# A two-layer hybrid decoder: the diagonal of linear attention as an elementwise product, small matmuls on all 128 rows, and other code for the first and the last norm

## The chip, the cores and the metric

The kernel runs on one core of one Trainium2 chip. The metric is the time of one execution on the device, in microseconds (us).

## The reference

The input x has 512 tokens of 1024 channels in float32. There are two layers. Each adds a mixer (a state-space scan, "SSD"; gated linear attention, "GLA"; dilated window attention; all three fed by one input projection and merged by sigmoid gates) and a gated MLP with a short convolution. An RMSNorm stands before each of these and at the end. Comments at the right are added here.

```python
def rmsnorm(x, w):
    xf = x.astype(jnp.float32)
    y = xf * lax.rsqrt(jnp.mean(xf * xf, axis=-1, keepdims=True) + RMS_EPS)
    return (y * w.astype(jnp.float32)).astype(x.dtype)

def gla_chunked(q, k, v, log_a):                 # q, k: 4 heads of 64; v: 4 heads of 128
...
    bcum = jnp.cumsum(log_a.reshape(bsz, nc, C, nh, dk), axis=2)
    causal = jnp.tril(jnp.ones((C, C), dtype=bool))
    diff = bcum[:, :, :, None] - bcum[:, :, None, :]
    decay = jnp.exp(jnp.where(causal[:, :, None, None], diff, -jnp.inf))
    scores = jnp.einsum('bcthd,bcshd,bctshd->bchts', q, k, decay)
    o_intra = jnp.einsum('bchts,bcshe->bcthe', scores, v)
...
def gla_mixer(q, k, v, gate_lr, r, gate_w, gate_b, norm_w):
...
    pre = gate_lr.astype(f32) @ gate_w.astype(f32) + gate_b.astype(f32)   # 16 rows to 256
    log_a = (jax.nn.log_sigmoid(pre) / GLA_TAU).reshape(bsz, seq, GLA_HEADS, GLA_DK)
    o = gla_chunked(qh, kh, vh, log_a)
...
def hybrid_mixer(hn, ...):
    proj = hn @ w_in.astype(hn.dtype)
    (z, xbc, dt_raw, gq, gk, gv, g_lr, g_r, qkv, gates) = jnp.split(...)
    y_ssd = ssd_mixer(z, xbc, dt_raw, ...)       # dt_raw: 16 columns
    y_gla = gla_mixer(gq, gk, gv, g_lr, g_r, ...)
    y_att = dilated_attention_mixer(qkv)
    merged = (gates[:, :, 0] * (y_ssd @ wb_ssd) + gates[:, :, 1] * (y_gla @ wb_gla)
              + gates[:, :, 2] * (y_att @ wb_att))
    return merged @ w_out.astype(hn.dtype)
...
def reference(x, ...):
    for l in range(DEPTH):                       # 2
        x = x + hybrid_mixer(rmsnorm(x, norm1_w[l]), ...)
        x = x + conv_ffn(rmsnorm(x, norm2_w[l]), ...)
    return rmsnorm(x, final_norm_w)
```

In the scores of GLA a token's own term (t = s) has decay 1, so the diagonal of the scores is the sum over d of q[t,d] * k[t,d].

## The kernel before

**Layout.** Activations lie with channels on the 128 partitions and the 512 tokens along the free side: x is eight tiles of 128x512 (xs). float32 products of full size are done in three passes of a rounded format: each operand is split into a high part (wh, xh) and the remainder (wl, xl), and `mm3` issues high by high, low by high, high by low. All weights are read in the order of use as 374 units of 128x1024 (`weight_plan`). `fetch` loads a unit, `parts` splits it (cast wh on ACT, subtraction wl on DVE), `unit` hands it to the projection that uses it; a unit is split two units ahead, and there are three buffers of wh and of wl, so a cast waits until PE is through with an older unit. A unit is 24 matmuls of 128x512.

**Order.** The order on PE is that of the code: the large matmuls of a unit are queued in a list (`large`), and each small matmul, issued by `mm` or `transpose`, is followed by one large one. Work beside the projections is written as generators (`side`), which are advanced by `tick` when a unit's matmuls have been queued; a generator says by `yield n` after how many units it wants to go on. The rows of ACT, DVE, POOL and SP are placed by the framework's scheduler; each engine works its row in order. Small matmuls are plain float32, and a profile shows each as two passes.

**The places of the change.** `small_proj` makes gd: rows 0 to 15 are the low-rank input of the GLA gate, rows 32 to 47 the raw step sizes of SSD; the other rows of the weight unit are zero. `gla_decay` multiplies rows 0 to 15 with the gate weights gw. `ssd_decay` transposes rows 32 to 47, four blocks of 128 tokens. `gla_pair` handles two heads (64 rows each); there are two pairs in a layer, started one unit apart. It begins with five clears on DVE (suf, two ksb, two qsb) and the diagonal: eight products of k and q over the 64 rows of a head, masked with the identity into S; later levels write the blocks below the diagonal into S.

`norm_stats` sums the squares by matmuls with ones, `factors` computes the reciprocal root (three Newton steps on 128x4 or 128x8 tiles) and four diagonal tiles dg; one unit later `norm_side` broadcasts the factors to all partitions by a matmul of ones with dg and copies them to rstdB. `first` loads x and makes the first split and the squares. The last norm does the same without a side, multiplies each tile of x by the broadcast in PSUM on DVE, and writes it out from two queues, ACT's (even tiles) and SP's (odd).

Of the kernel before, what the change touches and what calls it, by code (L numbers as in the profile page):

```python
# [11 lines left out]
F32 = mybir.dt.float32  # L12
# [84 lines left out]
def shape_constants():  # L97
# [22 lines left out]
    is_b = (i[:, None] // 32 == np.arange(4)[None, :]).astype(f)  # L120
    own = np.stack([is_r, is_b], axis=1)
    own64 = np.concatenate([i[:, None] % 16 == np.arange(16)[None, :],
                            i[:, None] % 64 // 16 == np.arange(4)[None, :]], axis=1).astype(f)
    lev = np.zeros((P, 7, 64), f)
    for n in range(7):
        L = 1 << n
# [10 lines left out]
def hybrid_decoder(ctx: ExitStack, tc: tile.TileContext, ins, out):  # L137
# [19 lines left out]
    def big(shape, dt=F32, n="b"):  # L157
        return big_p.tile(shape, dt, tag="b", name=nm(n))
# [128 lines left out]
    def blk(c):  # L287
        return slice(c * P, (c + 1) * P)
# [12 lines left out]
    for l in range(depth):  # L301
        pcs.append(cp.tile([P, N_PC], F32, name=f"pc{l}"))
        rows.append(cp.tile([P, 48], F32, name=f"rows{l}"))
        gws.append(cp.tile([16, 256], F32, name=f"gw{l}"))
    fnw = cp.tile([P, KD], F32, name="fnw")
    ident, tri, strict = mats[:, 0], mats[:, 1], mats[:, 2]
    own64 = cp.tile([P, 20], F32, name="own64")
    own_c = cp.tile([P, 4, P], F32R, name="own_c")
    ones = cp.tile([P, P], F32, name="ones")
    V.memset(ones, 1.0)  # L310

    def constants():
        for t, n in ((mats, "mats"), (own64, "own64"), (amask, "amask"), (sel, "sel"), (own, "own"), (fnw, "fnw")):
            nc.sync.dma_start(out=t, in_=ins[n])
        for l in range(depth):
            if l:
                nc.sync.dma_start(out=pcs[l], in_=ins["pc"][l])
            nc.sync.dma_start(out=rows[l], in_=ins["rows"][l].partition_broadcast(P))
            nc.sync.dma_start(out=gws[l], in_=ins["gw"][l])
        levf = big([P, 7, 64], n="levf")  # L320
        nc.sync.dma_start(out=levf, in_=ins["lev"])
        for n in range(7):
            V.tensor_copy(lev[:, n].rearrange("p (c i) -> p c i", c=4), levf[:, n:n + 1].to_broadcast([P, 4, 64]))
        V.tensor_copy(own_c, own64[:, 16:20].unsqueeze(2).to_broadcast([P, 4, P]))
# [38 lines left out]
    def norm_stats(acc, both):  # L363

        n = 8 if both else 4
        ss = mx()
        for c in range(n):
            mm(ss[:, c:c + 1], acc[:, blk(c) if c < 4 else res(c - 4)], ones[:, 0:1], True, True)
        return factors(ss, n)

    def factors(ss, n):
        t = sml([P, n])
        V.tensor_scalar(t, ss[:, :n], 1.0 / D, EPS, ALU.mult, ALU.add)
        rsqrt(rs[:, :n], t, n)
        if n == 8:
            V.tensor_scalar(hr, rs[:, :4], 0.5, None, ALU.mult)
        dg = big([P, T], n="dg")
        for c in range(4):
            V.tensor_scalar(dg[:, blk(c)], ident, rs[:, c:c + 1], None, ALU.mult)
        return dg  # L380

    def norm_side(acc, both):
        dg = norm_stats(acc, both)
        yield 1
        b = mx()
        mm(b, ones, dg, True, True)
        A.copy(rstdB, b)


    def attention(yh, yl, pre):  # L390
# [144 lines left out]
    def small_proj():  # L535
        o = pp()
        proj_cm(o, xhl, "small")
        gd = big([64, T], n="gd")
        V.tensor_mul(gd, o[:64], rstdB[:64])
        return gd  # L540


    def gla_decay(l, gd, las):
        pc, gw = pcs[l], gws[l]
        for m in range(2):
            o = mx()
            mm(o, gw[:, blk(m)], gd[:16], True, True)
            p0, p1 = big([P, T], n="p0"), big([P, T], n="p1")
            V.tensor_scalar(p0, o, pc[:, O_GB + m:O_GB + m + 1], None, ALU.add)
            V.tensor_scalar(p1, p0, 0.0, None, ALU.min)  # L550
            V.scalar_tensor_tensor(p0, p1, 2.0, p0, ALU.mult, ALU.subtract)
            las.append((p0, p1))
# [38 lines left out]
    def gla_pair(m, qk, cum, vt, wt, pc, yh, yl):  # L591
# [7 lines left out]
        hp = [slice(0, 64), slice(64, 128)]  # L599
        S = [big([P, 2, 2, P], n="S") for _ in range(2)]  # L600
        X = []
        for j in range(2):
            o = mx()
            for c in range(4):
                mm(o[:, blk(c)], k[hp[j], blk(c)], q[hp[j], blk(c)], True, True)
            for x in range(2):
                V.tensor_mul(S[x][:, :, j], o[:, 256 * x:256 * x + 256].rearrange("p (c t) -> p c t", c=2),
                             ident.unsqueeze(1).to_broadcast([P, 2, P]))
        for n in range(9):
            L = 1 << n  # L610
            G = 256 // L
# [81 lines left out]
    def ssd_decay(l, gd, dec):  # L693
# [3 lines left out]
        A.activation(nA, rw[:, 16:32], AF.Exp)  # L697
        o = mx()
        for c in range(4):
            transpose(o[:, 16 * c:16 * c + 16], gd[32:48, blk(c)], ident[32:48, 32:48])  # L700
        pre = sml([P, 4, 16], n="pre")
        V.tensor_add(pre, o[:, :64].rearrange("p (c h) -> p c h", c=4), rw[:, :16].unsqueeze(1).to_broadcast([P, 4, 16]))
        pre = pre.rearrange("p a b -> p (a b)")
        mn = sml([P, n], n="mn")
        V.tensor_scalar(mn, pre, 0.0, None, ALU.min)
# [343 lines left out]
    for c in range(4):  # L1049
        mm(ss[:, c:c + 1], sq[:, blk(c)], ones[:, 0:1], False, c == 3)  # L1050
    A.activation(xs[KD - 1], xs[KD - 1], AF.Copy, scale=fnw[:, KD - 1:KD])
    dg = factors(ss, 4)
    b = mx()
    mm(b, ones, dg, True, True)
    for m in range(KD):
        V.tensor_mul(xs[m], xs[m], b)  # L1056
        (nc.sync if m % 2 else A).dma_start(out=out[:, m], in_=xs[m])
    assert pos[0] == len(plan)

# [58 lines left out]
```

## Time and profile before

| what | value |
|---|---|
| median of 3 runs | 2325.44 us (2324.39 to 2331.16) |
| profiled execution, its own time | 2324.64 us |
| its span, first to last instruction | 2322.8 us |
| mean granted TensorE clock | 0.997 |
| busy: PE, PEld, DVE, ACT, POOL | 99%, 83%, 61%, 39%, 0% |
| matmuls (passes) | 10776 |
| read from HBM | 200.35 MB |

Busy time of PE is modelled from pipelined matmuls, so steps between starts say more than durations. An operation's row has its start, its duration, engine, line, operation, names (out<-in), shape and count; what stands in brackets is the idle time of the engine before it and what ended that. Matmuls and weight loads (PEld) are listed apart.

### The profile page before, as it was taken

The numbers are of one execution on the slowest core, as the hardware profiler recorded it, in microseconds if no ns is written. First come the engines' busy times: TensorE is split into PE (matmuls) and PEld (weight loads), VectorE is DVE, ScalarE is ACT, GpSimd is POOL, SyncE is SP. The second block draws the span as 40 slices with busy tenths as digits, with TensorE's granted clock in tenths as the row PEclk, the third lists the DMA queues.
The fourth block names the chain that finished last, engine by engine and source line by source line (L and its number), as shares of the span: only waits on it lengthen the run. The fifth ranks groups of instructions, "written<-read, shape, count | busy, mean of one in ns | idle before, by whom it ended". The sixth has DMA issues, their size and how long they took to land.

```text
span 2322.8 us, 27385 instructions
## 1 busy us (share of the span) xinstructions
PE 2299.9 (99%) x10776; PEld 1918.3 (83%) x10776; DVE 1412.0 (61%) x2511; ACT 901.9 (39%) x1487; POOL 0.2 (0%) x4
## 2 busy tenths in 40 slices
PE   8999999999999999999999999999999999999997
PEld 7888878888888888888898888788888888888886
DVE  4467548687865566654325764686888556665533
ACT  4344423445443333332224444234454433333321
POOL 0000000000000000000000000000000000000000
PEclk9999999999999999999999999999999999999998
DMA  5322222222223333233333222222222233333331
GB/s 180 102 82 75 80 64 91 76 71 73 82 75 98 92 98 97 94 100 96 95 91 100 82 82 68 74 85 73 73 73 82 82 94 97 95 97 100 95 96 54
DMA packets 58512, 204.21 MB, mean 88 GB/s; under 512 B 7152, under 2 KB 7824, under 8 KB 58384
## 3 DMA queue, kind: packets, MB, share of 16 engines
q1 hardware_dynamic: 57808, 201.42, 28.3%
q8 instruction: 84, 1.38, 0.2%
q10 hardware_dynamic: 576, 1.05, 0.1%
q14 instruction: 44, 0.36, 0.1%
HBM read 200.35 MB, written 2.10 MB: 87 GB/s over the span
## 4 chain that ended last, share of the span: by engine, by line
PE 98%; DVE 1%; ACT 0%; DMA 0%; issue 0%; DVEq 0%; SPq 0%; ACTq 0%
PE pp L178 77%; PE pp L183 11%; PE mx L186 8%; PE mx L190 1%; DVE wl L251 0%; DVE x L1056 0%; DVE cv L762 0%; DMA x<-in_xT 0%; DVE xD L821 0%; DVE th L905 0%; DVE th L930 0%; DVE xe L823 0%; DVE xdt L820 0%; ACT th L906 0%; ACT cx L765 0%
## 5 line engine op out<-in xcount | busy, mean ns | idle before, releaser
L249 ACT CAST wh<-raw 128x1024 fp32r<-128x1024 f32 x374 | 393.0, 1051 | 960.8 <-PE pp L178 738.7
L251 DVE TENSOR_TENSOR wl<-raw,wh 128x1024 fp32r<-128x1024 f32 x374 | 457.4, 1223 | 368.7 <-ACT wh L249 363.4
L178 PE MATMUL pp<-xh,wl 128*128 128x512 f32 x1582 | 616.7, 390 | 0.0
L178 PE MATMUL pp<-xl,wh 128*128 128x512 f32 x1556 | 605.9, 389 | 0.0
L178 PE MATMUL pp<-xh,wh 128*128 128x512 f32 x1504 | 586.5, 390 | 0.0
L178 PEld LDWEIGHTS pp<-xh,wl 128*128 128x128 f32 x1582 | 297.0, 188 | 62.9 <-issue 1.0
L178 PEld LDWEIGHTS pp<-xl,wh 128*128 128x128 f32 x1556 | 292.3, 188 | 60.6 <-issue 0.5
L178 PEld LDWEIGHTS pp<-xh,wh 128*128 128x128 f32 x1504 | 282.3, 188 | 60.1 <-DVE wl L251 1.5
L178 PE MATMUL pp<-wh,xh 128*128 128x512 f32 x372 | 147.1, 395 | 7.8 <-ACT wh L249 7.8
L178 PE MATMUL pp<-wh,xl 128*128 128x512 f32 x392 | 154.5, 394 | 0.0
L178 PE MATMUL pp<-wl,xh 128*128 128x512 f32 x386 | 152.5, 395 | 0.5 <-DVE wl L251 0.5
L183 PE MATMUL pp<-xh,wh 128*128 128x512 f32 x304 | 148.0, 487 | 0.0
L178 PE MATMUL pp<-hh,wl 128*128 128x512 f32 x352 | 136.9, 389 | 0.0
L178 PE MATMUL pp<-hh,wh 128*128 128x512 f32 x352 | 136.9, 389 | 0.0
L178 PE MATMUL pp<-hl,wh 128*128 128x512 f32 x352 | 136.9, 389 | 0.0
L758 DVE TENSOR_TENSOR cx<-pp,rstdB 128x512 f32<-128x512 f32 x76 | 52.4, 689 | 121.1 <-PE pp L178 120.9
L183 PE MATMUL pp<-xl,wh 128*128 128x512 f32 x252 | 124.3, 493 | 0.0
L183 PE MATMUL pp<-xh,wl 128*128 128x512 f32 x226 | 110.5, 489 | 0.0
L765 ACT ACTIVATE cx<-cv 128x512 f32<-128x512 f32 x76 | 48.1, 633 | 139.5 <-DVE cv L762 138.6
L178 PEld LDWEIGHTS pp<-wh,xh 128*128 128x128 f32 x372 | 85.8, 231 | 17.6 <-ACT wh L249 7.8
L178 PEld LDWEIGHTS pp<-wh,xl 128*128 128x128 f32 x392 | 89.8, 229 | 10.5
L178 PEld LDWEIGHTS pp<-wl,xh 128*128 128x128 f32 x386 | 88.6, 230 | 11.4 <-DVE wl L251 1.0
(267 smaller groups left out, 3381.6 us busy)
## 6 DMA issues: line engine op xcount, KB each, us to landing
raw<-in_wall SPq DMA_DIRECT2D x374, 512.0 KB, 3.6
x<-in_xT SPq DMA_DIRECT2D x8, 256.0 KB, 5.9
out_dram<-x ACTq DMA_DIRECT2D x4, 256.0 KB, 2.4
out_dram<-x SPq DMA_DIRECT2D x4, 256.0 KB, 2.5
cosR<-in_rope SPq DMA_DIRECT2D x2, 256.0 KB, 4.5
sinR<-in_rope SPq DMA_DIRECT2D x2, 256.0 KB, 4.6
amask<-in_amask SPq DMA_DIRECT2D x1, 256.0 KB, 5.3
levf<-in_lev SPq DMA_DIRECT2D x1, 224.0 KB, 3.2
```

Of the source, the lines that this page charges most:

```text
L178: PE.matmul(o, lhsT=l, rhs=r, start=start, stop=stop)
L183: PE.matmul(o, lhsT=l, rhs=r, start=start, stop=stop)
L186: PE.matmul(o, lhsT=l, rhs=r, start=start, stop=stop)
L190: PE.transpose(o, i, idn)
L249: A.copy(h, r)
L251: V.tensor_sub(lo, r, f(h))
L758: V.tensor_mul(x, o, rstdB)
L765: A.activation(x, v, AF.Tanh)
```

## The change

The diagonal of a pair is now the product gqk = q * k (128x512, on DVE), summed over the 64 rows of each head by four matmuls against two columns that mark the heads (own64, columns 20 and 21). The sums are copied (dia) and multiplied with the identity into S. gd is made with all 128 rows, the gate product uses all of them against gw padded with zero rows, and the SSD step sizes are transposed as full 128x128 blocks. The factors of a norm are broadcast by four matmuls whose weights are a column of rs repeated 128 times (`spread`), and dg goes. At the start one small activation stands first on ACT, and eleven 128x128 products of ones first on PE. In the last norm ACT copies the broadcast to bs, and POOL multiplies two of the eight tiles.

```diff
--- before.py
+++ after.py
@@ -120,7 +120,8 @@
     is_b = (i[:, None] // 32 == np.arange(4)[None, :]).astype(f)
     own = np.stack([is_r, is_b], axis=1)
     own64 = np.concatenate([i[:, None] % 16 == np.arange(16)[None, :],
-                            i[:, None] % 64 // 16 == np.arange(4)[None, :]], axis=1).astype(f)
+                            i[:, None] % 64 // 16 == np.arange(4)[None, :],
+                            i[:, None] // 64 == np.arange(2)[None, :]], axis=1).astype(f)
     lev = np.zeros((P, 7, 64), f)
     for n in range(7):
         L = 1 << n
@@ -301,13 +302,19 @@
     for l in range(depth):
         pcs.append(cp.tile([P, N_PC], F32, name=f"pc{l}"))
         rows.append(cp.tile([P, 48], F32, name=f"rows{l}"))
-        gws.append(cp.tile([16, 256], F32, name=f"gw{l}"))
+        gws.append(cp.tile([P, 256], F32, name=f"gw{l}"))
     fnw = cp.tile([P, KD], F32, name="fnw")
     ident, tri, strict = mats[:, 0], mats[:, 1], mats[:, 2]
-    own64 = cp.tile([P, 20], F32, name="own64")
+    own64 = cp.tile([P, 22], F32, name="own64")
     own_c = cp.tile([P, 4, P], F32R, name="own_c")
     ones = cp.tile([P, P], F32, name="ones")
     V.memset(ones, 1.0)
+
+    warm = cp.tile([P, 1], F32, name="warm")
+    A.activation(warm, ones[:, 0:1], AF.Tanh)
+    wm = mx()
+    for _ in range(11):
+        PE.matmul(wm[:, :P], lhsT=ones, rhs=ones, start=True, stop=True)
 
     def constants():
         for t, n in ((mats, "mats"), (own64, "own64"), (amask, "amask"), (sel, "sel"), (own, "own"), (fnw, "fnw")):
@@ -316,7 +323,8 @@
             if l:
                 nc.sync.dma_start(out=pcs[l], in_=ins["pc"][l])
             nc.sync.dma_start(out=rows[l], in_=ins["rows"][l].partition_broadcast(P))
-            nc.sync.dma_start(out=gws[l], in_=ins["gw"][l])
+            V.memset(gws[l], 0.0)
+            nc.sync.dma_start(out=gws[l][:16], in_=ins["gw"][l])
         levf = big([P, 7, 64], n="levf")
         nc.sync.dma_start(out=levf, in_=ins["lev"])
         for n in range(7):
@@ -366,7 +374,7 @@
         ss = mx()
         for c in range(n):
             mm(ss[:, c:c + 1], acc[:, blk(c) if c < 4 else res(c - 4)], ones[:, 0:1], True, True)
-        return factors(ss, n)
+        factors(ss, n)
 
     def factors(ss, n):
         t = sml([P, n])
@@ -374,17 +382,17 @@
         rsqrt(rs[:, :n], t, n)
         if n == 8:
             V.tensor_scalar(hr, rs[:, :4], 0.5, None, ALU.mult)
-        dg = big([P, T], n="dg")
+
+    def spread():
+        b = mx()
         for c in range(4):
-            V.tensor_scalar(dg[:, blk(c)], ident, rs[:, c:c + 1], None, ALU.mult)
-        return dg
+            mm(b[:, blk(c)], rs[:, c:c + 1].to_broadcast([P, P]), ident, True, True)
+        return b
 
     def norm_side(acc, both):
-        dg = norm_stats(acc, both)
+        norm_stats(acc, both)
         yield 1
-        b = mx()
-        mm(b, ones, dg, True, True)
-        A.copy(rstdB, b)
+        A.copy(rstdB, spread())
 
 
     def attention(yh, yl, pre):
@@ -535,8 +543,8 @@
     def small_proj():
         o = pp()
         proj_cm(o, xhl, "small")
-        gd = big([64, T], n="gd")
-        V.tensor_mul(gd, o[:64], rstdB[:64])
+        gd = big([P, T], n="gd")
+        V.tensor_mul(gd, o, rstdB)
         return gd
 
 
@@ -544,7 +552,7 @@
         pc, gw = pcs[l], gws[l]
         for m in range(2):
             o = mx()
-            mm(o, gw[:, blk(m)], gd[:16], True, True)
+            mm(o, gw[:, blk(m)], gd, True, True)
             p0, p1 = big([P, T], n="p0"), big([P, T], n="p1")
             V.tensor_scalar(p0, o, pc[:, O_GB + m:O_GB + m + 1], None, ALU.add)
             V.tensor_scalar(p1, p0, 0.0, None, ALU.min)
@@ -599,13 +607,16 @@
         hp = [slice(0, 64), slice(64, 128)]
         S = [big([P, 2, 2, P], n="S") for _ in range(2)]
         X = []
-        for j in range(2):
-            o = mx()
-            for c in range(4):
-                mm(o[:, blk(c)], k[hp[j], blk(c)], q[hp[j], blk(c)], True, True)
-            for x in range(2):
-                V.tensor_mul(S[x][:, :, j], o[:, 256 * x:256 * x + 256].rearrange("p (c t) -> p c t", c=2),
-                             ident.unsqueeze(1).to_broadcast([P, 2, P]))
+        qk = big([P, T], n="gqk")
+        V.tensor_mul(qk, q, k)
+        o = mx()
+        for c in range(4):
+            mm(o[:, 2 * c:2 * c + 2], qk[:, blk(c)], own64[:, 20:22], True, True)
+        dia = sml([P, 4, 2], n="dia")
+        V.tensor_copy(dia, o[:, :8].rearrange("p (c j) -> p c j", j=2))
+        for x in range(2):
+            V.tensor_mul(S[x], ident.unsqueeze(1).unsqueeze(1).to_broadcast([P, 2, 2, P]),
+                         dia[:, 2 * x:2 * x + 2].unsqueeze(3).to_broadcast([P, 2, 2, P]))
         for n in range(9):
             L = 1 << n
             G = 256 // L
@@ -697,9 +708,9 @@
         A.activation(nA, rw[:, 16:32], AF.Exp)
         o = mx()
         for c in range(4):
-            transpose(o[:, 16 * c:16 * c + 16], gd[32:48, blk(c)], ident[32:48, 32:48])
+            transpose(o[:, blk(c)], gd[:, blk(c)], ident)
         pre = sml([P, 4, 16], n="pre")
-        V.tensor_add(pre, o[:, :64].rearrange("p (c h) -> p c h", c=4), rw[:, :16].unsqueeze(1).to_broadcast([P, 4, 16]))
+        V.tensor_add(pre, o.rearrange("p (c h) -> p c h", c=4)[:, :, 32:48], rw[:, :16].unsqueeze(1).to_broadcast([P, 4, 16]))
         pre = pre.rearrange("p a b -> p (a b)")
         mn = sml([P, n], n="mn")
         V.tensor_scalar(mn, pre, 0.0, None, ALU.min)
@@ -1049,11 +1060,15 @@
     for c in range(4):
         mm(ss[:, c:c + 1], sq[:, blk(c)], ones[:, 0:1], False, c == 3)
     A.activation(xs[KD - 1], xs[KD - 1], AF.Copy, scale=fnw[:, KD - 1:KD])
-    dg = factors(ss, 4)
-    b = mx()
-    mm(b, ones, dg, True, True)
-    for m in range(KD):
-        V.tensor_mul(xs[m], xs[m], b)
+    factors(ss, 4)
+    b = spread()
+    bs = big([P, T], n="bs")
+    A.copy(bs, b)
+    for m in (0, 2, 1, 3, 4, 5, 6, 7):
+        if m in (2, 5):
+            nc.gpsimd.tensor_mul(xs[m], xs[m], bs)
+        else:
+            V.tensor_mul(xs[m], xs[m], b)
         (nc.sync if m % 2 else A).dma_start(out=out[:, m], in_=xs[m])
     assert pos[0] == len(plan)
```

On PE, at the first pair of the first layer (pp is the sum of the unit in hand, xh, xl and wh, wl the parts of x and of the weights; mx is a small result). Before:

```order
L178 MATMUL pp_2418<-wh_2451,xl_118 128x512
L186 MATMUL mx_2588<-gq_2103,gk_2136 128x128
L183 MATMUL pp_2569<-xh_103,wh_2481 128x512
L186 MATMUL mx_2588<-gq_2103,gk_2136 128x128
L183 MATMUL pp_2569<-xl_111,wh_2481 128x512
```

After:

```order
L187 MATMUL mx_2604<-own_99,gqk_2602 128x2
L184 MATMUL pp_2583<-xh_117,wh_2495 128x512
L187 MATMUL mx_2604<-own_99,gqk_2602 128x2
L184 MATMUL pp_2583<-xl_125,wh_2495 128x512
L187 MATMUL mx_2604<-own_99,gqk_2602 128x2
L184 MATMUL pp_2583<-xh_117,wl_2497 128x512
L187 MATMUL mx_2604<-own_99,gqk_2602 128x2
L184 MATMUL pp_2583<-xh_118,wh_2495 128x512
L191 MATMUL mx_2624<-mats,gd_1993 128x128
L184 MATMUL pp_2583<-xl_126,wh_2495 128x512
```

Products of gqk stand where those of gq and gk stood, four for eight, in front of all large matmuls of the unit.

On DVE, at the same pair. Before:

```order
L598 MEMSET ksb_2578 128x512
L598 MEMSET ksb_2579 128x512
L598 MEMSET qsb_2580 128x512
L598 MEMSET qsb_2581 128x512
L607 TENSOR_TENSOR S_2586<-mx_2588,mats 128x2x128
L607 TENSOR_TENSOR S_2587<-mx_2588,mats 128x2x128
L607 TENSOR_TENSOR S_2586<-mx_2599,mats 128x2x128
L607 TENSOR_TENSOR S_2587<-mx_2599,mats 128x2x128
```

After, and then (behind the line of dots) at the second pair:

```order
L252 TENSOR_TENSOR wl_2588<-raw_2463,wh_2586 128x1024
L606 MEMSET ksb_2592 128x512
L606 MEMSET ksb_2593 128x512
L606 MEMSET qsb_2594 128x512
L606 MEMSET qsb_2595 128x512
L611 TENSOR_TENSOR gqk_2602<-gq_2117,gk_2150 128x512
...
L252 TENSOR_TENSOR wl_2685<-raw_2493,wh_2683 128x1024
L732 SCALAR_TENSOR_TENSOR p_2647<-p_2647,z_2643 128x64
L606 MEMSET ksb_2690 128x512
L606 MEMSET qsb_2691 128x512
L606 MEMSET qsb_2692 128x512
L611 TENSOR_TENSOR gqk_2699<-gq_2203,gk_2236 128x512
```

The product gqk has come in behind the clears, where the masking of the finished matmuls stood.

On ACT, at the end of the program (x_84 is tile 0 of x, x_86 tile 2). Before:

```order
L1051 ACTIVATE x_91<-x_91,fnw 128x512
L1057 DMA out_dram<-x_84 128x512
L1057 DMA out_dram<-x_86 128x512
L1057 DMA out_dram<-x_88 128x512
L1057 DMA out_dram<-x_90 128x512
```

After:

```order
L1062 ACTIVATE x_91<-x_91,fnw 128x512
L1066 COPY bs_17579<-mx_17574 128x512
L1072 DMA out_dram<-x_86 128x512
L1072 DMA out_dram<-x_84 128x512
L1072 DMA out_dram<-x_88 128x512
L1072 DMA out_dram<-x_90 128x512
```

The copy to bs is new, and tile 2, one of POOL's two, is now first in ACT's queue. In SP's queue tile 5, POOL's other one, has come in front of tiles 1, 3 and 7.

## Rows read from the trace of the kernel before

**Rows 1.** The page: its first line, and the chain of work that ended last, by engine.

```profile
span 2322.8 us, 27385 instructions
...
PE 98%; DVE 1%; ACT 0%; DMA 0%; issue 0%; DVEq 0%; SPq 0%; ACTq 0%
```

**Rows 2.** The timeline of PE around the two GLA pairs of the first layer: start, duration, engine, line, operation, out<-in, tile of the array (rows*columns), shape, count.

```profile
320.79 0.39 PE L178 MATMUL pp<-wh,xl 128*128 128x512 f32 x1
321.10 0.48 PE L186 MATMUL mx<-gq,gk 64*128 64x128 f32 x2
...
321.95 0.48 PE L186 MATMUL mx<-gq,gk 64*128 64x128 f32 x2
...
327.85 0.23 PE L190 MATMUL mx<-mats,gd 16*128 16x16 f32 x1
...
328.45 0.23 PE L190 MATMUL mx<-mats,gd 16*128 16x16 f32 x1
...
332.96 0.49 PE L186 MATMUL mx<-gq,gk 64*128 64x128 f32 x2
...
343.24 0.38 PE L186 MATMUL mx<-qsb,ksb 128*128 128x128 f32 x2
```

**Rows 3.** The same timeline at small matmuls of 128 rows with one large matmul after each (the third small one is a single pass, a transpose), and a stretch of large matmuls alone near the end, its first and its last row (55 matmuls).

```profile
364.41 0.38 PE L186 MATMUL mx<-qsb,ksb 128*128 128x128 f32 x2
...
364.86 0.27 PE L190 MATMUL mx<-mats,ac 128*128 128x128 f32 x1
...
365.21 0.40 PE L178 MATMUL pp<-yah,wl 128*128 128x512 f32 x1
...
2293.07 0.39 PE L178 MATMUL pp<-hh,wl 128*128 128x512 f32 x1
...
2305.31 0.39 PE L178 MATMUL pp<-hh,wl 128*128 128x512 f32 x1
```

**Rows 4.** The timeline of DVE at the first pair.

```profile
322.68 0.48 DVE L594 MEMSET suf<- 128x512 f32 x1
323.08 1.16 DVE L251 TENSOR_TENSOR wl<-raw,wh 128x1024 fp32r<-128x1024 f32 x1
324.30 1.03 DVE L598 MEMSET ksb<- 128x512 f32 x2
325.38 1.03 DVE L598 MEMSET qsb<- 128x512 f32 x2
326.32 0.69 DVE L607 TENSOR_TENSOR S<-mx,mats 128x256 f32<-128x256 f32 x2
```

**Rows 5.** The timelines of ACT and of DVE behind the first pair's unit: a cast that waits for PE, and a subtraction wl.

```profile
332.84 1.05 ACT L249 CAST wh<-raw 128x1024 fp32r<-128x1024 f32 x1 [10.00 <-PE pp L178]
...
346.92 1.22 DVE L251 TENSOR_TENSOR wl<-raw,wh 128x1024 fp32r<-128x1024 f32 x1
```

**Rows 6.** The timeline of PE at the gate product of the first layer (two products, four passes) and the large matmul behind it.

```profile
253.35 1.98 PE L186 MATMUL mx<-gd,gw 16*128 16x512 f32 x4
255.26 0.50 PE L178 MATMUL pp<-xh,wh 128*128 128x512 f32 x1
```

**Rows 7.** The timeline at the start of the program, all engines.

```profile
4.77 1.28 ACT L349 ACT_TABLE_LOAD   x1 [4.77 <-DMA x<-in_xT]
...
6.70 1.03 ACT L249 CAST wh<-raw 128x1024 fp32r<-128x1024 f32 x1
...
9.04 0.79 PE L178 MATMUL pp<-wl,xh 128*128 128x512 f32 x1 [0.47 <-DVE wl L251]
...
9.48 0.62 ACT L354 ACTIVATE acc<-x 128x512 f32<-128x512 f32 x1
...
13.04 0.58 PE L178 MATMUL pp<-wl,xh 128*128 128x512 f32 x1
...
13.46 0.39 PE L178 MATMUL pp<-wh,xl 128*128 128x512 f32 x1
...
24.63 0.68 DVE L358 TENSOR_TENSOR acc<-acc,sq 128x512 f32<-128x512 f32 x1
```

**Rows 8.** The timeline of PE at the sums of the first norm; each row is one product in two passes with a large matmul after it. From 29.13 on the weights are every fourth column of acc.

```profile
27.32 0.28 PE L186 MATMUL mx<-ones,acc 128*128 128x1 f32 x2
...
29.13 0.40 PE L186 MATMUL mx<-ones,acc 128*128 128x1 f32 x2
...
29.71 0.40 PE L186 MATMUL mx<-ones,acc 128*128 128x1 f32 x2
```

**Rows 9.** Stretches at the end: length, busy time (and instructions) of PE, PEld, DVE, ACT and POOL, granted TensorE clock, mean share of the DMA engines, GB/s.

```profile
2308.00:2309.00 1.00, 0.92 (x8) 0.84 (x8) 0.04 (x1) 0.57 (x1) 0.00 (x0) 1.00 0.00 0
...
2310.00:2311.00 1.00, 0.00 (x0) 0.00 (x0) 0.83 (x6) 0.00 (x0) 0.00 (x0) 0.80 0.00 0
2311.00:2312.00 1.00, 0.00 (x0) 0.00 (x0) 0.93 (x6) 0.00 (x0) 0.00 (x0) 0.50 0.00 0
...
2317.00:2319.00 2.00, 0.00 (x0) 0.00 (x0) 2.00 (x4) 0.00 (x0) 0.00 (x0) 0.50 1.02 383
```

**Rows 10.** The timeline at the end: the broadcast of the last norm, the products with it, the first of the output transfers.

```profile
2312.26 2.08 PE L186 MATMUL mx<-dg,ones 128*128 128x512 f32 x2 [3.34 <-DVE dg L379]
2314.38 4.87 DVE L1056 TENSOR_TENSOR x<-x,mx 128x512 f32<-128x512 f32 x8 [2.17 <-PE mx L186]
2315.09 3.92 ACTq L1057 DMA_DIRECT2D out_dram<-x  x4
```

## The prediction

> **What bounds the kernel now.** I read the page first: the span, and the chain that ended last, which lies on PE for 98% [rows 1]. So a microsecond counts only where PE issues or waits. Next I read PE's row of instructions at the code that changes. One large matmul (128x512) takes 0.227 us: 54 steps from 2293.07 to 2305.31 [rows 3]. Small matmuls are laid between large ones, so a small one's price is the step over the pair less 0.227.
>
> At the diagonal of linear attention a step takes 0.85 us (321.10 to 321.95), so one 64-row product costs 0.62 us [rows 2]. A small product that fills 128 rows has steps of 0.45 and costs 0.228 [rows 3]. A 16-row transpose has steps of 0.60 and costs 0.37 [rows 2], a 128-row one 0.35 and 0.12 (364.86 to 365.21) [rows 3]. Few rows are dear here, and the change removes them. Then I asked what the new matmuls wait for, on DVE [rows 4, 5].
>
> **The diagonal and the transposes.** Between 321.02 (0.227 after the last large matmul) and 343.24, PE issues two weight units of 24 large matmuls, 16 products of 64 rows and 4 transposes: 22.2 us [rows 2]. Afterwards the first unit holds 24 large, 4 products of two columns (I take the 128-row price, 0.228: fewer columns make a product no cheaper, since the norm's one-column products, with steps of 0.58, cost even 0.35 [rows 8]) and 4 full transposes: 5.44 + 0.91 + 0.48 = 6.83. The second holds 24 and 4: 6.35. That is 13.2, so PE has 9.0 us less to do per layer, 18.0 in all.
>
> The Trainium skill, page "TensorE: Matmul & The Clock Gate", section "Why this matters for your kernels", says that one matmul of 32 rows takes the same time as one of 128; by that the transposes and the gate product below would gain nothing, and the sum would be 2.2 us higher. The trace does not agree: 0.37 against 0.12.
>
> **The new wait.** The old products read q and k, long ready. The new ones read gqk, a DVE product, and in DVE's row it stands behind five clears and the low part of a weight unit. In the rows of before DVE is busy without a gap here: clear 322.68, wl 323.08, clears of ksb and qsb from 324.30 to 326.32, where the first diagonal product starts [rows 4]. None of that moves earlier. gqk takes about 0.68, as a sum of two 128x512 operands does [rows 7], so it ends at 327.0. PE arrives at 321.02 and has nothing else it may do: all large matmuls stand behind it. Wait: 6.0 us.
>
> The second pair is late in a chain that begins when PE ends the first unit, at T. DVE's th reads that unit's sums; the wh cast waits for a buffer that this unit reads to its end (in before the cast starts at 332.84 and the next unit's first product at 332.96) and takes 1.05 [rows 2, 5]. th runs beneath it; wl begins at T+1.1 and takes 1.2; then stand five clears (0.40 to 0.51 each, 2.3) [rows 4], three small steps of the decay chain between them (0.2 each) and gqk (0.68): T+5.8. PE is at T. Wait: 5.8 us. Before, the second pair read nothing that was late. I bound this wait by 5.2 (small steps hidden) and 6.5 (where at full clock DVE is behind by the decay chain, 13 small operations with an exponential on ACT between).
>
> So the four waits of two layers are 23.6 us. They alone exceed the 18.0.
>
> **The clock.** The rows show PE idle for some time only at the end: its last matmuls lie in 2308 to 2309, and the granted clock is 0.80 in 2310 to 2311 and 0.50, the level of 1.2 GHz, in 2311 to 2312 [rows 9]. The fall came some 2 us into that idle; a wait here is three times that. What a return costs the start shows, although the records grant 1.00 there: large matmuls are 0.42 apart up to 13.46 and 0.227 after, and unbroken from 9.04 [rows 7]. 4.4 us at half speed lose about 2.15 us. Bounds per wait: 0 (the clock holds) and 2.8 (counted from the first matmul at about 7.8, when wh is cast). I take 2.15, because the restart has a full queue as that start had: 8.6 for four. The second wait comes some 8 us after the first, so the clock rises and falls again.
>
> **The other edits.** (a) The gate product with all rows: four passes take 1.91 us from 253.35 to 255.26 [rows 6]; in full-row products a pass of 128 columns is 0.114 (half of 0.228), so four passes of 512 are 1.82: -0.1 each, -0.2 in all. (b) The spread: four products of 128 columns replace one of 512, and by the same price both are 0.91. With weights read at a step of four, as in the norm's later sums, a product is 0.58 - 0.23 = 0.35 (29.13 to 29.71) [rows 8], four 1.4. A repeated column stays at one address, nearer to contiguous weights: 0 for the four inner norms, upper bound +2.0. The four diagonal tiles that DVE drops are worth nothing inside: the spread is issued a weight unit, some 5.4 us, after the sums, and that covers them; without this cover they would be 0.9 per norm.
>
> (c) The start. The table load, 1.28 from 4.77, moves ahead of the first x; a square of 0.62 (now at 9.48) comes in before the wh cast at 6.70 [rows 7]. Net 0.6 us earlier. The eleven added products are 22 passes of twice 0.114 at half speed, 5.0 us from about 1.0 on; they end 1.1 before wh. If they hold the clock up, another 2 us. But PE then arrives at the norm's sums before acc: acc's last addition ends at 25.31 [rows 7], which lets the first of those products start near 25.55 after its weights' load, against 27.32 [rows 8]. The gain stops at 1.75. I take 1.2, bounds 0.6 and 1.75. The clears of gw run while DVE waits for pc.
>
> (d) The end. Dropping the diagonal tiles, which with the root's last steps fill DVE in 2311 to 2312 [rows 9], brings the broadcast from 14.34 to about 13.45 (eight passes of 128 columns at half clock are the same columns) [rows 10]. Now the copy to bs and one POOL product come before the first output transfer, as ACT's queue has x2 in front and SP's has x5. Before, the first left at 2315.09 and the bytes then flowed at 383 GB/s with the engines' share at 1.02 [rows 9, 10]: the end is that first issue plus 7.7 us, and DVE's two saved products lie beneath. Copy 0.6, as the square of the same size; POOL has no such row, so its bounds are DVE's sum, 0.68, and twice DVE's 128x1024 wl, 2.4; I take 1.22, one wl. First issue 15.35: +0.2, from -0.3 to +1.4.
>
> The page "GPSIMD Engine Reference", section 3.1, of the Trainium skill gives about 2.6 cycles at 1.2 GHz per element for two inputs; the estimate from it is 1.1 us, which makes the sum 0.1 lower. No run here shows it yet.
>
> **Sum.** Waits +23.6, work -18.0, clock +8.6, gate -0.2, spread 0, start -1.2, end +0.2: +13.0. The profiled execution took 2324.64 us (span 2322.8 [rows 1]); the median of the three runs is 0.8 above it, well inside their spread. 2324.64 + 13.0 is 2337.6.
>
> **Rivals.**
>
> A, forecast: waits and half clock. 2337.6, 69%. Its own range is 2333 to 2345: all bounds at their dear end give +23.6 + 1.4 - 18.0 + 11.2 - 0.2 + 2.0 - 0.6 + 1.4 = +20.8.
>
> B: the clock holds, or falls in one wait only. For it: the idle at the end follows 2 us of thin work, while here PE was full just before. Against: the length of the wait. +13.0 - 8.6 = +4.4: 2329; 18%.
>
> C, faster: the products come in time. DVE would have to reach gqk 6 us sooner in each pair. It decides at 4.8 us: where wait and clock together stay under (18.0 + 1.2)/4 = 4.8 per pair, the kernel gains (1.2 is what the other edits give). With no wait at all it is 2324.64 - 19.2 = 2305; with only the first wait of each layer and the clock held, 2317. Against it is that DVE's row in front of gqk is unchanged and gapless. 10%.
>
> D: few rows cost no more than all, and their steps above come from something else. (So the page of the Trainium skill named above has it.) Then (transposes 4 x 0.25 per layer, gate 0.1) 2.2 us of the gains stay away: 2340. The measured steps speak against it; 3%.
>
> **Numbers.** About 0.3%, 7 us, is what a measurement of this kernel tells from no change. Slower by more: A, D and no more than a slip of B, 0.71. Within: B and the mild part of C, 0.20. Faster: 0.09. The range takes in B's centre and A's dear end, 2327 to 2345, and leaves out C.
>
> **What would show it.** PE's list of waits should have a new entry, mx for gqk, four times, 5.2 to 6.5 us each, and the granted clock 0.50 near 327, 341, 1474 and 1488. The unit's first pair should have steps near 0.45 at full clock, transposes 0.35. The list of the start should show PE's first large matmul near 7.1, and a short wait for acc near 25. The last writes should leave no earlier than 2314.8 in the old count. I am wrong if gqk starts before PE ends the unit, or if no row near the waits is below 1.00.

## The result and the profile after

The changed kernel takes 2343.4 us (median of 4 runs, 2342.91 to 2346.73); before, in the same comparison, takes 2325.84. The ratio is 1.0078, with a 95% interval of 1.0066 to 1.0091: slower by 0.7 to 0.9%, some 17.6 us. The profiled execution of after is its longest, 2346.73 us with a mean granted clock of 0.986; the other three have 0.989 and spans 3.3 to 3.8 us shorter.

PE's list of waits in the kernel after (line waited for, us in total, times, longest):

```profile
PE mx L187 <- DVE gqk L611: 23.2, 4, 5.8
PE pp L179 <- ACT wh L250: 2.5, 1, 2.5
PE mx L187 <- DVE rs L351: 2.4, 1, 2.4
```

The first line is new: before has no wait of PE at the pairs. PE's row at the two pairs of layer 1 (compare [rows 2]):

```profile
321.52 0.39 PE L179 MATMUL pp<-wh,xl 128*128 128x512 f32 x1
327.74 0.58 PE L187 MATMUL mx<-own,gqk 128*128 128x2 f32 x2 [5.83 <-DVE gqk L611]
...
328.75 0.42 PE L187 MATMUL mx<-own,gqk 128*128 128x2 f32 x2
...
329.61 0.42 PE L187 MATMUL mx<-own,gqk 128*128 128x2 f32 x2
...
344.08 0.59 PE L187 MATMUL mx<-own,gqk 128*128 128x2 f32 x2 [5.75 <-DVE gqk L611]
...
354.39 0.38 PE L187 MATMUL mx<-qsb,ksb 128*128 128x128 f32 x2
```

From the last large product's end (321.75, 0.227 behind its start) to the first score product (354.39) PE needs 32.6 us, where before needed 22.2 [rows 2]. Behind each wait the steps are 0.86 (328.75 to 329.61), not the 0.45 of a full clock. The granted clock in four stretches of 1 us (PE, PEld, DVE, ACT and POOL with counts, then clock, DMA share, GB/s):

```profile
324.00:325.00 1.00, 0.00 (x0) 0.00 (x0) 0.97 (x1) 0.01 (x1) 0.00 (x0) 0.98 0.03 8
325.00:326.00 1.00, 0.00 (x0) 0.00 (x0) 0.91 (x2) 0.00 (x0) 0.00 (x0) 0.50 0.01 4
334.00:335.00 1.00, 1.00 (x4) 0.81 (x3) 0.87 (x5) 0.26 (x1) 0.00 (x0) 0.50 0.00 0
335.00:336.00 1.00, 1.00 (x5) 0.77 (x5) 0.90 (x3) 0.00 (x0) 0.00 (x0) 0.90 0.00 0
```

It falls to 0.50 at 325.0, 3.2 us into the idle time, and returns at 335.2, when PE has worked again for 7.4 us. At the other three waits it falls in the same way (0.50 from 342.0, 1482.1 and 1499.1).

Where the 22.1 us of span came from: the casts of the 374 weight units can be compared one by one, since ACT's cast follows PE's release of a buffer. Unit 25's starts at 144.6 in before and 145.8 in after (+1.2: 0.4 at the first norm's sums, 0.5 at its spread, 0.3 in the weight units behind it, whose cause no run shows); across each layer's gate products the distance falls by 0.4; across the pairs of layer 1 it grows from 0.7 to 11.1, of layer 2 from 10.6 to 21.0; elsewhere, single casts apart, it moves by no more than 0.2; the last norm adds 1.2.

### The profile page after: what moved, and what is told of

The parts are those of the page before. It is cut to its first block, busy times and chain, and to the rows that moved or that the text cites. A ratio compares the mean times of both kernels' runs of the same rounds, so it can differ in the third digit from the quotient of the medians.

```text
span 2344.9 us, 27416 instructions
## 1 busy us (share of the span) xinstructions
PE 2302.7 (98%) x10796; PEld 1933.1 (82%) x10796; DVE 1415.3 (60%) x2491; ACT 902.4 (38%) x1489; POOL 2.7 (0%) x6
## 3 DMA queue, kind: packets, MB, share of 16 engines
q10 hardware_dynamic: 576, 1.05, 0.1%
## 4 chain that ended last, share of the span: by engine, by line
PE 97%; DVE 2%; ACT 0%; issue 0%; DMA 0%; SPq 0%; DVEq 0%; ACTq 0%
PE pp L179 76%; PE pp L184 11%; PE mx L187 8%; PE mx L191 2%; DVE wl L252 0%; DMA raw<-in_wall 0%; DVE gw L594 0%; DVE cv L773 0%; DVE qsb L606 0%; DVE ksb L606 0%; ACT wh L250 0%; DVE x L1071 0%; DVE gqk L611 0%; DVE xD L832 0%; DVE suf L602 0%
```

## The experiments

The before of each comparison has a median of 2324.7 to 2324.9 us; ratios are against it.

**e1_early: the product early.** After, with the product in `gla`, right behind k, and handed to `gla_pair`:

```diff
             V.tensor_mul(k, o, rstdB)
-            qk.append((q, k))
+            g = big([P, T], n="gqk")
+            V.tensor_mul(g, q, k)
+            qk.append((q, k, g))
...
-        q, k = qk
+        q, k, qk = qk
...
-        qk = big([P, T], n="gqk")
-        V.tensor_mul(qk, q, k)
```

> Kernel after, but gqk = q * k is multiplied right behind k's projection, some 50 us before the pair, so that PE's first diagonal product finds it ready. Theory A (four waits of 5.8 us and the half clock behind each are the whole loss, and the saving of work is real): no wait for gqk, granted clock 1.00 near both pairs of both layers, two weight units with their small products in 13.2 us where before takes 22.2 and after 32.6; 2325.8 - 18.0 of work - 0.6 of gate products + 2.0 of start and end = 2309. Rival D (few rows cost no more than all, no work was saved): the waits go, but the units still take some 20 us each layer; 2322 to 2327.

Measured: 2322.15 us, ratio 0.9989 (0.9979 to 0.9998). The waits for gqk are gone and the first unit of the pair runs as theory A has it, but the time is 13 us above theory A's 2309, at the edge of what rival D gave (2322 to 2327), though not for D's reason: the work is saved, as the rows show. Its PE, clock, DVE and ACT rows:

```profile
333.85 0.38 PE L187 MATMUL mx<-qsb,ksb 128*128 128x128 f32 x2
346.10 0.77 PE L187 MATMUL mx<-qsb,ksb 128*128 128x128 f32 x2 [5.72 <-DVE qsb L633]
```

```profile
344.00:345.00 1.00, 0.00 (x0) 0.00 (x0) 1.00 (x2) 0.00 (x0) 0.00 (x0) 0.50 0.86 225
350.00:351.00 1.00, 1.00 (x4) 0.77 (x3) 1.00 (x3) 0.00 (x0) 0.00 (x0) 0.59 0.00 0
```

```profile
328.95 0.85 DVE L633 TENSOR_TENSOR qsb<-gq,ex 64x256 f32<-64x256 f32 x2 [1.54 <-ACT ex L630]
329.98 0.68 DVE L916 TENSOR_TENSOR th<-pp,rstdB 128x512 f32<-128x512 f32 x1
...
335.10 0.20 DVE L722 TENSOR_SCALAR rd<-u 128x64 f32<-128x64 f32 x1 [1.91 <-ACT u L719]
343.90 1.29 DVE L618 TENSOR_TENSOR S<-mats,dia 128x512 f32<-128x512 f32 x2
345.11 0.84 DVE L633 TENSOR_TENSOR qsb<-gq,ex 64x256 f32<-64x256 f32 x2
```

```profile
333.86 1.05 ACT L250 CAST wh<-raw 128x1024 fp32r<-128x1024 f32 x1 [2.54 <-PE pp L179]
334.82 0.25 ACT L719 ACTIVATE u<-u 128x64 f32<-128x64 f32 x1
```

PE reaches the pair's end 9.0 us sooner against before (the next unit's cast: from 0.4 ahead to 9.4 ahead), and then stands 5.7 us in front of the second pair's first query block. DVE's row there is clears, decay steps and the masked S, and a stand of 1.91 us for ACT's exponential u, which ACT worked only behind a cast that waited for PE. The clock falls again (0.50 from 344.0 to 350.8). Of the 9.0 us, 8.2 are given back. So neither theory was complete: the saving is real, and a second wait stood behind the first. I call the new theory B: DVE's row up to qsb is the next limit.

**e2_filler: work in place of the wait.** After, with products whose results are not used, ahead of the diagonal's:

```diff
         V.tensor_mul(qk, q, k)
         o = mx()
+        for _ in range(24):
+            PE.matmul(o[:, 128:256], lhsT=ident, rhs=ident, start=True, stop=True)
```

> Kernel after, with 24 products of the identity with itself (128x128, results unused) ahead of the four diagonal products of each pair: PE works for 24 * 0.228 = 5.5 us where it waited 5.8, and what it waits for comes no earlier. Theory A (the half clock follows from the idle time): granted clock 1.00 near the pairs, the wait becomes 5.5 us of work and 0.3 of idle, and only the clock's share goes: the profiled execution of after lost 3.7 to 4.1 us to it behind each wait, so some 12 to 16 of 2343.4 go: 2328 to 2332. Rival (the thin products, or something else near the pairs, take the clock down): the clock still falls; 2342 to 2344.

Measured: 2332.34 us, ratio 1.0029 (1.0018 to 1.0041), 0.3 above the dear end of theory A. PE works through the stretch in which after stood, and the clock is 1.00 there:

```profile
325.00:326.00 1.00, 1.00 (x11) 1.00 (x10) 0.91 (x2) 0.00 (x0) 0.00 (x0) 1.00 0.12 33
```

```profile
327.65 0.38 PE L187 MATMUL mx<-own,gqk 128*128 128x2 f32 x2 [0.47 <-DVE gqk L611]
```

gqk comes no earlier (behind PE's arrival 6.0 and 6.4 us, in after 6.0 and 5.9), and still 11 us of 2343.4 are gone: the price of the half clock by itself, over four waits, by the medians is some 11, or 12 if the 0.5 that the second gqk of each layer comes later is counted. In after's profiled execution it was more: PE worked 7.4 to 8.2 us at half clock behind each wait, which loses 3.7 to 4.1 us, 15.6 in all.

**e3_first: the product ahead of the clears.**

```diff
+        qk = big([P, T], n="gqk")
+        V.tensor_mul(qk, q, k)
         suf = big([P, T], n="suf")
         V.memset(suf, 0.0)
...
-        qk = big([P, T], n="gqk")
-        V.tensor_mul(qk, q, k)
```

> Kernel after, but within a pair gqk is multiplied ahead of the five clears, which gives up none of the cover in front of the pair. DVE's row then has gqk right behind the last gate product of the first pair and behind th, a low part and two small steps in the second. Theory A: the first wait shrinks from 5.8 to 2.3 us, the second to 3.2 (1.1 to the cast's end, 1.2 of wl, 0.2, 0.7), 12 us of waits go. In after the clock fell some 3.2 us into the idle; if it holds in both pairs, 2319; if it falls in the second of each layer alone, 2325; if it falls in all, 2331. Rival (the clears are not what gqk stood behind): waits stay over 5 us, 2340 or more.

Measured: 2326.3 us (2324.67 to 2329.45), ratio 1.0007 (0.9999 to 1.0016). The waits are those of theory A:

```profile
322.24 0.38 PE L187 MATMUL mx<-own,gqk 128*128 128x2 f32 x2 [2.10 <-DVE gqk L602]
332.27 0.59 PE L187 MATMUL mx<-own,gqk 128*128 128x2 f32 x2 [2.91 <-DVE gqk L602]
```

```profile
332.00:333.00 1.00, 0.73 (x3) 0.73 (x4) 0.94 (x5) 0.00 (x0) 0.00 (x0) 0.57 0.35 66
338.00:339.00 1.00, 1.00 (x4) 0.81 (x3) 0.23 (x1) 0.00 (x0) 0.00 (x0) 0.52 0.00 0
```

In layer 1 the clock held behind the wait of 2.10 and fell behind that of 2.91; in layer 2, with waits of the same length, it fell behind both. The time lies between the forecasts for a fall at two waits (2325) and at four (2331). So shortening a wait to 2 or 3 us saves the wait's length, and not surely the clock.

**e5_pool and e5c_order: DVE relieved.** e5_pool is e1_early with

```diff
-        V.memset(suf, 0.0)
+        nc.gpsimd.memset(suf, 0.0)
         for t in ksb + qsb:
-            V.memset(t, 0.0)
+            nc.gpsimd.memset(t, 0.0)
```

and e5c_order also moves the copy dia and the two masked products S behind level 0's qsb and ksb.

> The kernel with the early product (e1_early), and the five clears of each pair on POOL instead of DVE. Theory B (PE's work at the pairs is saved, but DVE's row up to the second pair's first query block qsb is the next limit: in e1_early PE stood there 5.7 us per layer, and behind that the clock was half for 6.8 us): about 2.0 us of clears leave DVE's row between the first and second pair, the wait for qsb falls from 5.7 to 3.5 or so: 2322.2 - 2 * 2.2 = 2318, or 2311 if the clock then holds too. Rival (the wait is set by something else than DVE's row, such as ACT's exponentials): 2322, wait unchanged.

> As e5_pool, and in a pair the blocks qsb and ksb of level 0 are written ahead of the copy dia and the two masked products S, so that DVE's row has the second pair's qsb in front of the decay chain's steps and of S. Theory B: no wait at the pairs over 1 us, clock 1.00 there; in e1_early the cast of the next weight unit stood 9.0 us per layer ahead of before's and gave 8.2 back; these stay: 2322.2 - 2 * 8.2 = 2306. Rival: what was saved is waited for at the next level of the pair, and little comes of it; 2315 to 2322.

Measured: e5_pool 2306.7 us, ratio 0.9922 (0.9909 to 0.9936); e5c_order 2306.89 us, ratio 0.9922 (0.9909 to 0.9934). e5_pool's PE row, and in DVE's row the first pair's qsb, th and the second pair's qsb:

```profile
320.07 0.28 PE L187 MATMUL mx<-own,gqk 128*128 128x2 f32 x2
...
333.31 0.38 PE L187 MATMUL mx<-qsb,ksb 128*128 128x128 f32 x2
...
339.68 0.38 PE L187 MATMUL mx<-qsb,ksb 128*128 128x128 f32 x2
```

```profile
324.27 0.84 DVE L633 TENSOR_TENSOR qsb<-gq,ex 64x256 f32<-64x256 f32 x2
...
327.12 0.69 DVE L916 TENSOR_TENSOR th<-pp,rstdB 128x512 f32<-128x512 f32 x1 [1.56 <-PE pp L179]
...
338.37 0.85 DVE L633 TENSOR_TENSOR qsb<-gq,ex 64x256 f32<-64x256 f32 x2
```

The two units take 13.24 us (320.07 to 333.31) with no wait, and qsb is done at 339.22, 0.5 us ahead of PE. That bears out theory B, but the gain, 15.5 us against e1_early, is more than I expected of the clears: qsb stands 6.7 us earlier than in e1_early (345.11 to 338.37), some 0.5 of it because the whole kernel is there earlier. From th to qsb DVE needs 11.25 us instead of 15.13, and the 1.91 us in which it stood for ACT's exponential are among what went, so a half of these 3.9 us is not the clears' own time, and the rival (ACT's exponential) had a part of the truth; th itself starts some 2.3 us sooner: ahead of it stands the first pair's qsb, which in e1_early came at 328.95, behind the clears and an exponential on ACT, and here at 324.27. The reordering in e5c_order adds nothing.

**e8_ctrl: the clears alone.** Before with e5_pool's diff and nothing else.

> Kernel before, with the five clears of each pair on POOL alone; its diagonal of 16 products of 64 rows stays. Control for e5_pool. Theory B (DVE's row limits the pairs only once PE's work there is small): before has no wait of PE at the pairs, so no change: 2324.9, within 0.2%. Rival (the clears alone are what e5_pool gained by, with or without the new diagonal): 2310 to 2318.

Measured: 2324.91 us, ratio 1.0 (0.9991 to 1.001). DVE's relief is worth nothing as long as PE has 22.2 us of work at the pairs.

**e7_rows: the full rows alone.** Before with the edits of gd, gw and the transposes.

> Kernel before, with the full rows alone: gd of 128 rows, the gate product over all of them with gw padded by zeros, full transposes. No product gqk, no other edit. Forecast's prices: eight transposes at 0.12 instead of 0.37 us, and gate products that took 0.4 us less per layer in after: -2.8 us, 2322.1, none of it waited for. Rival D (few rows cost no more than all): 2324.9, steps of 0.60 at the transposes as before.

Measured: 2321.51 us, ratio 0.9985 (0.9976 to 0.9994): 3.3 us, where the steps had priced 2.8. The casts run 1.0 further ahead across the pairs of each layer, where the transposes stand, and 0.4 across the gate products. The transposes have steps of 0.35:

```profile
327.05 0.27 PE L190 MATMUL mx<-mats,gd 128*128 128x128 f32 x1
...
327.40 0.27 PE L190 MATMUL mx<-mats,gd 128*128 128x128 f32 x1
```

Rival D is out. What makes few rows dear between large matmuls, the rows themselves or the change of the array's tile (16*128 or 64*128 in [rows 2], 128*128 around them), no run separates.

**e4_start: the start alone.** Before with the small activation and the eleven products of ones.

> Kernel before, with the start of after alone (the small activation first on ACT, eleven products of ones first on PE). Forecast's step: -1.2 us at the norm's first sum (26.1 instead of 27.32). Theory now, from after's trace (sum at 27.71, the clock half until 14.2): +0.4 at that sum, and no other difference in the program; a time within 0.1% of before.

Measured, in one execution: 2327.4 us, against a median of 2324.9. Neither figure held. PE's row and two stretches:

```profile
6.90 0.50 PE L178 MATMUL pp<-wh,xh 128*128 128x512 f32 x1 [0.79 <-ACT wh L249]
...
26.10 0.38 PE L186 MATMUL mx<-ones,acc 128*128 128x1 f32 x2 [1.58 <-DVE acc L364]
```

```profile
26.00:27.00 1.00, 0.90 (x6) 0.83 (x6) 1.00 (x2) 0.00 (x0) 0.00 (x0) 0.80 0.87 299
36.00:37.00 1.00, 1.00 (x4) 0.75 (x3) 0.00 (x0) 0.58 (x1) 0.00 (x0) 0.57 0.00 0
```

Here the products of ones end at 6.10, PE stands only 0.8 us before the first weights, and large products run at full rate from the start. PE reaches the norm's first sum at 24.5, 2.8 us before [rows 8], waits 1.58 us for acc, and then the clock is half from 26.6 to 36.9: 3 us later than before by the next casts. In after the products took 4.16 us instead of 5.06, PE then stood 2.47 us, and the clock fell there (0.50 from 7.5 to 14.3):

```profile
1.05 4.16 PE L317 MATMUL mx<-ones 128*128 128x128 f32 x22 [1.05 <-DVE ones L311]
7.68 0.80 PE L179 MATMUL pp<-wh,xh 128*128 128x512 f32 x1 [2.47 <-ACT wh L250]
```

```profile
3.00:4.00 1.00, 1.00 (x7) 1.00 (x7) 0.11 (x1) 0.00 (x0) 0.00 (x0) 1.00 0.92 205
4.00:5.00 1.00, 1.00 (x10) 1.00 (x9) 0.00 (x0) 0.23 (x1) 0.00 (x0) 1.00 0.91 369
...
7.00:8.00 1.00, 0.32 (x1) 0.29 (x1) 0.34 (x1) 1.00 (x2) 0.00 (x0) 0.76 1.01 356
...
14.00:15.00 1.00, 1.00 (x6) 0.77 (x5) 0.99 (x2) 0.94 (x1) 0.00 (x0) 0.83 0.85 244
```

The same start stands in six more traces, and PE's stand and its first sum differ from one to the next: with stands of 2.0 to 2.5 us (after, e2_filler, e6_best) the first sum comes at 27.5 to 27.7, with stands of 1.0 to 1.7 (e1_early, e3_first, e5_pool, e5c_order) at 25.9 to 26.6. The clock fell in all seven, but in the last four it was back by 11.3 to 13.0.

**e6_best and e9_best2: start and end mended.** e6_best is e5c_order with lev loaded and cast six units later, and in the last norm

```diff
-    bs = big([P, T], n="bs")
-    A.copy(bs, b)
-    for m in (0, 2, 1, 3, 4, 5, 6, 7):
-        if m in (2, 5):
-            nc.gpsimd.tensor_mul(xs[m], xs[m], bs)
-        else:
-            V.tensor_mul(xs[m], xs[m], b)
+    for m in range(KD):
+        V.tensor_mul(xs[m], xs[m], b)
```

e9_best2 is e5_pool with these two edits and 18 products of ones.

> As e5c_order, with two more edits. The masks lev are loaded and cast after the first norm, so that DVE's row has the last sums of acc with nothing of lev between them; and in the last norm neither copy to bs nor POOL: DVE multiplies all eight tiles from PSUM in the order of the tiles. Theory: where the eleven products hold the clock, PE reaches the norm's first sum near 24.5 us (e4_start), and acc is there now: about 2.9 us before the kernel before; and the first output transfer leaves 1.3 us earlier behind the last large product than in e1_early. With e5c_order's 2306: 2302. If the clock at the start comes back late, as in the kernel after: 2305.

> As e5_pool, with the later masks lev and the last norm without copy and POOL of e6_best, and 18 instead of 11 products of ones at the start. With eleven, PE stood 2.0 to 2.5 us before the first weights in after and e6_best and the clock was half until 14 us; in e4_start it stood 0.8 and the clock held. Theory: seven more products end at 6.8 to 7.7 us, next to the first weights; the clock holds; PE reaches the norm's first sum near 24.5 and finds acc: -2.9 us against before; last norm 16.6 us behind the last large product as in e6_best: 2306.7 - 2.0 - 1.3 = 2303. If the clock falls at the start all the same: 2305 to 2306.

Measured: e6_best 2305.62 us, ratio 0.9918 (0.9904 to 0.9932); e9_best2 2302.71 us, ratio 0.9905 (0.989 to 0.9919). In e6_best the clock fell at the start as in after. In e9_best2 it holds, and PE finds acc ready (one trace, with the masks lev moved as well):

```profile
1.05 6.09 PE L317 MATMUL mx<-ones 128*128 128x128 f32 x36 [1.05 <-DVE ones L311]
...
24.56 0.28 PE L187 MATMUL mx<-ones,acc 128*128 128x1 f32 x2
```

The sum at 24.56 is 2.8 us ahead of before's 27.32 [rows 8]. From the last large product to the end e6_best takes 16.6 us, e1_early 17.9, before 17.5. e9_best2 is the fastest kernel here, 22 us below before.

## Why the prediction came out, step by step

The forecast was +13.0 us, 2337.6, and measured are +17.6, 2343.4. The waits and the half clock are the reason, as forecast A had it. The range, 2327 to 2345, held the median with 1.6 us to spare, and the profiled execution (2346.73) lies above it; that the range held owes something to luck, for in the trace the clock cost more than its dear bound.

**The new wait**: right. Forecast 6.0 and 5.8 us, measured 5.83 and 5.75 in both layers; 23.2 in all against 23.6. (The list counts from the modelled end of the last product. Counted as the forecast did, from 0.227 behind its start, they are 5.99 and 5.91, 23.8 in all.) e3_first shows that it was the clears and wl in DVE's row that gqk stood behind.

**The work of PE**: right. Forecast 13.2 us for two units with their small products; 13.24 in e5_pool, where nothing is waited for. After has the same work within 0.3: 32.6 less 11.9 of waits (by the forecast's count) less some 7.8 of half clock is 12.9. The Trainium skill, page "TensorE: Matmul & The Clock Gate", section "Why this matters for your kernels", has it that one matmul of 32 rows takes the same time as one of 128. The trace does not agree here: steps of 0.60 became 0.35, and e7_rows gained 3.3 us from rows alone.

**The clock**: the mechanism was right, the size was the term that failed. "I take 2.15, because the restart has a full queue as that start had" should have been 3.7 to 4.1 per wait in the profiled execution; even the dear bound, 2.8, was too low. 8.6 forecast, 15.6 there; by the medians it is some 11 to 12 (e2_filler), 2.8 to 3.0 per wait. The start's rows had given 4.4 us at half speed, the pairs' have 7.4 to 8.2 after the restart; no run here settles why they differ.

**The start**: forecast -1.2, measured +0.4 (27.71 against 27.32) in after's trace; the same start in four of the later traces came 0.8 to 1.4 earlier than before, near the forecast. The table load's move was real (0.73, not 4.77), but the cast of wh then waited 0.57 us for its data, and the products of ones ended 2.5 us before PE's first large product, not 1.1: the forecast took half speed for all of them, and they came to full rate in the fifth microsecond (7 passes in one, 10 in the next). They did not hold the clock: large products ran at half rate to 14.3, before's to 13.5 [rows 7]. That PE would arrive ahead of acc was right only where the clock held (e4_start), and there the forecast left out that the clock can fall behind a wait of 1.58 us.

**The spread**: 0 was right for three of the four inner norms, the dear bound for the first:

```profile
35.50 0.38 PE L187 MATMUL mx<-mats,rs 128*128 128x128 f32 x2
...
36.07 0.38 PE L187 MATMUL mx<-mats,rs 128*128 128x128 f32 x2
...
820.17 0.38 PE L187 MATMUL mx<-mats,rs 128*128 128x128 f32 x2
...
820.63 0.38 PE L187 MATMUL mx<-mats,rs 128*128 128x128 f32 x2
```

Steps of 0.57 in the first, 0.46 in the others: +0.5 in all. Why the first differs stays open.

**The gate product**: forecast -0.1 each, measured -0.4 (by the casts).

**The end**: forecast +0.2, measured +1.2. PE, DVE and POOL in after:

```profile
2328.76 1.87 PE L187 MATMUL mx<-ones,sq 128*128 128x1 f32 x8 [1.38 <-ACT sq L1056]
2333.06 2.08 PE L187 MATMUL mx<-mats,rs 128*128 128x128 f32 x8 [2.43 <-DVE rs L351]
...
2335.79 3.67 DVE L1071 TENSOR_TENSOR x<-x,mx 128x512 f32<-128x512 f32 x6 [2.79 <-ACT bs L1066]
2335.84 2.50 POOL L1069 TENSOR_TENSOR x<-x,bs 128x512 f32<-128x512 f32 x2 [2335.40 <-ACT bs L1066]
```

The sums of sq took 1.87, not 1.05, because the clock was half already from 2328.6; in e1_early, where it was not, the end costs +0.4, near the forecast. POOL's product took 1.25 us, forecast 1.22. The estimate from the Trainium skill, page "GPSIMD Engine Reference", section 3.1 (about 2.6 cycles per element for two inputs), was 1.1, and the trace is 0.15 above it. What I missed: DVE's first product waits for ACT's copy of the same PSUM tile, though the broadcast it reads is done at 2335.14; in e6_best, without the copy, it starts at 2295.37, 0.04 behind the broadcast's end.

**The rivals.** B is out for the kernel after, since the clock fell at all four waits. D is out by e7_rows. C's mechanism, no wait, gives 2306.7 in e5_pool with its price of 2305; but "with no wait at all" hid a step. I asked what PE would wait for first, and not what stood behind it: without the wait for gqk alone the kernel is at 2322 (e1_early). Against 2337.6 the profiled execution of after is 9.1 us higher: clock +7.0, start +1.6, end +1.0, spread +0.5, gate products -0.6, waits -0.4, each good to some 0.3. The median is 5.8 higher. Some 2.5 to 3.5 of that are the clock's by e2_filler, and before's median in this comparison lies 1.2 above the execution with which the sum began (2324.64); how the rest divides in executions without a trace is not shown.

## What to carry over

Before work is taken off the bounding engine, look at how full the row of its feeder is in the same stretch: here DVE's had 14.9 busy us of PE's 22.2, in one chain, and less PE work alone turned into waits, first for the product and then for the block behind it. A wait of PE can be charged twice, once by its length and once by the half clock behind it (all waits of 2.9 us or more at the pairs, and one of the two of 2.10). So it pays to make the operand early, to take off the feeder's row what an idle engine can do (worth 15.5 us behind the early product, nothing without it), and to count what the next wait will be. A warm-up that leaves a gap in front of the real work can lose the clock again (in seven of eight traces with eleven products); the one that reached up to it (18 products) kept it, and the first sum came 2.8 us ahead of before.

## What was not expected of the hardware

The half clock, once it had fallen, lasted 6.8 to 10.3 us from fall to return at the pairs and at the sums (e1_early 344.0 to 350.8, e4_start 26.6 to 36.9, after 325.0 to 335.2), with PE busy again for most of it, and 3.4 at some starts (e5_pool 8.2 to 11.6). Behind a wait of 2.10 us it fell in one layer of e3_first and not in the other. That kernel's times spread over 5 us, and they go with the mean granted clock: 2324.67 to 2326.3 at 0.993, 2327.66 to 2329.45 at 0.991. Eleven equal products of ones took 4.16 us in after and 5.06 in e4_start, though the granted clock reads 1.00 in both; the passes per microsecond show that PE came to full rate at 4 us in after and not before 6 in e4_start. At the start of the program, go by the steps and not by the granted clock.
